# A one-core hybrid decoder layer: the last token block loaded and squared whole, the inverse roots' steps issued together, the parameter load on ScalarE's queue, and a new order of the projection jobs

## The chip, the cores and the metric

The kernel runs on one core of a Trainium2 chip. The metric is the device time of one execution in microseconds. The time of a kernel is the median of several runs; the kernel before took 1043.09 us (three runs, 1042.55 to 1043.57).

## The reference, cut to what matters

x has 512 tokens of 2048 features. One layer normalises x, projects it to 7824 columns, and feeds three token mixers; their gated outputs are joined, projected back, added to x and normalised again.

```python
h = _rmsnorm(x, norm_w[l])
p = h @ w_in[l]
y_a = _rwkv7_mix(...)   # 16 heads of 64: a chain over chunks of 64 tokens, then a norm over each head
y_b = _moba_mix(...)    # 4 heads of 128: causal softmax attention
y_c = _gla_mix(...)     # 4 heads: chunked linear attention with decay, then a norm over each head
mix = jnp.concatenate([y_a, y_b, y_c], axis=-1)
x = x + mix @ w_out[l]
return _rmsnorm(x, final_norm_w)
```

The first norm needs, for each token, the inverse root of the mean square of its 2048 features (`rstd`). The kernel projects the raw x (times the norm's weights) and multiplies each projected tile by `rstd` when it is taken out of PSUM.

## The kernel before, in words

**The stream.** TensorE runs one long stream of 128x128 by 128x512 products at float32 accuracy: weights and activations are each split into a high and a low part, and three products (high-high, high-low, low-high) replace one. 62 *jobs* of 128 output columns (`low` has 16) make the input projection: a job has 16 k-tiles, so 48 products. Then the output projection has four column blocks (`cb`) of 192 products. The first three jobs of `ORDER` run side by side, a quarter at a time, while x arrives.

**Banks.** Jobs take four PSUM banks (`gb`) in turn. So a job can begin only when the job four places before it in `ORDER` has been taken out of its bank (`evac`, line 378, a multiplication by `rstd` on VectorE). Each job is taken out by one particular step of the mixers (`wait_free`, line 1259, waits for it, and `force`, line 333, then runs mixer steps with no products between them).

**Side work.** The mixers are Python generators. `pump` (line 325) is called after every three products and lets each generator whose last step is thought to be finished issue its next step. What is "finished" comes from a clock of estimated costs (`Clock`, line 62), so the estimates and `ORDER` fix the program of every engine: the hardware then runs each engine's instructions in that order. Four other PSUM banks (`sbk`) serve the side work. The side work on TensorE that uses part of the array (64x64, 128x64, 32x32 operands, line 129) appears as short bursts in the stream; `bank` (line 351) may hold a step back for up to 4 us of the estimated clock to let it join a burst of its own form.

**The mixers' order.** RWKV runs four pairs of heads in turn (`rwkv(q)`, q = 0 to 3): preparation of `k` and `r` jobs, `a_stage`, `solve`, then `chain(q)` of eight chunks with three dependent bursts each, then `group_norm(q)`. `a_stage` of q waits for the end of `group_norm(q-1)` (flag `finish`), and that for the gate jobs `ga` of q-1. GLA (`gla(0)`, `gla(1)`) and then the attention heads (`moba(0)` to `moba(3)`) run one after the other in `others` (line 1044). `moba(h)` takes out `mq`, `mk` and `mv` of its head; `moba_gate(h)` (line 1037) takes out `mg` of head h only after head h-1 is done.

**The token norm.** `load` with kind "sq" (line 1123) loads a block of 128 tokens of x, untransposed; `square` (line 1151) squares it on ScalarE with a sum per token. Blocks 0 to 2 lie in one tile of 128x2048 each; block 3 lies in four tiles of 128x512 (`fb[0]` to `fb[3]`), has four loads and four squares, and its four sums go through `small`. `stats` (line 403) waits for the four squares, adds the four sums of block 3 (line 407), yields, then runs `rsqrt` (line 395: a scale and shift on VectorE, a power of -1/2 on GpSimd), transposes the result four times on TensorE (line 414) and copies it out to `rstd_b`. `rsqrt` serves the mixers' norms too; its GpSimd estimate is 0.1 us + 0.17 us per column.

**The start.** The parameters (line 1237) are the first load on the queue of the sync engine (SP), which issues almost all loads. The first activation on ScalarE needs them as a scale.

Of the kernel before, what the change touches and what calls it, by code (L numbers as in the profile page):

```python
# [12 lines left out]
AF = mybir.ActivationFunctionType  # L13
# [3 lines left out]
S, D = 512, 2048  # L17
# [5 lines left out]
NORM_EPS = 1e-6  # L23
# [13 lines left out]

ORDER = """wdad k0 k1 ga1 r0 ga0 r1 v0 gq0 low v1 gv0 gk0 k2 gg0 gv1 gg1 k3 r2 ga2 r3 gq1 v2 gk1 gg2 gv2 ga3 v3 gv3 gg3 k4 mq0 mk0 k5 r4 r5 ga4 v4 v5 mv0 mg0 k7 mq1 mk1 mg1 ga5 k6 mv1 r6 r7 mq2 ga6 mg2 v6 mk2 mv2 v7 mv3 mq3 mk3 ga7 mg3"""  # L40
FIRST = {"wdad": C_WD, "low": C_LOW, "k": C_K, "r": C_R, "v": C_V, "ga": C_GA, "gq": C_QC, "gk": C_KC, "gv": C_VC,
         "gg": C_GC, "mq": C_QB, "mk": C_KB, "mv": C_VB, "mg": C_GB}

# [1 line left out]
def first_column(job):  # L45
    kind = job.rstrip("01234567")
    return FIRST[kind] + 128 * int(job[len(kind):] or 0)


JOBS = [(n, first_column(n)) for n in ORDER.split()]  # L50

# [50 lines left out]
def tile_hybrid(ctx: ExitStack, tc: tile.TileContext, x, xT, wu, wlow, wout, par, cst, w2a2_d, aup_d, fw, out):  # L102
    nc = tc.nc
    ck = Clock()

    pool = ctx.enter_context(tc.tile_pool(name="main", bufs=1))
# [4 lines left out]
    def sb(name, shape, dt=F32, tag=None):  # L111
        t_ = pool.tile(list(shape), dt, name=name, tag=tag or name)
        return t_

    def numel(ap):
        n = 1
        for s in ap.shape[1:]:
            n *= s
        return n
# [15 lines left out]
    def tr(o, i):  # L135
        ck.pe(0.0925, "f")
        k = i.shape[0]
        nc.tensor.transpose(o, i, ident[:k, :k])  # L138

    def dcost(*aps):  # L140
        ps = any(a.space == bass.MemoryType.PSUM for a in aps if hasattr(a, "space"))
        return ((120 if ps else 60) + numel(aps[0])) / 960
# [14 lines left out]
    def ts(o, a, s1, s2, op0, op1=None):  # L157
        ck.add("dve", dcost(o, a) / 1.6)
        if op1 is None:
            nc.vector.tensor_scalar(o, a, s1, None, op0=op0)  # L160
        else:
            nc.vector.tensor_scalar(o, a, s1, s2, op0=op0, op1=op1)  # L162

    def vcopy(o, a):
        ck.add("dve", dcost(o, a) / 1.6)
        nc.vector.tensor_copy(o, a)  # L166

    def red(o, a, op=ALU.add):
        ck.add("dve", dcost(a, o))
        nc.vector.tensor_reduce(o, a, axis=AX.X, op=op)  # L170

    def act(o, a, f, bias=None, scale=None, accum=None, dep=0.0):
        t = TABLES.get(f)
        cost = 0.1 + numel(a) * 0.00084 + 0.1 * ((bias is not None) + (scale is not None))
        if t is not None and t != ck.table:
            ck.table = t
            cost += 1.3
        end = ck.add("act", cost, dep)
        kw = {}
        if bias is not None:  # L180
            kw["bias"] = bias
        if scale is not None:
            kw["scale"] = scale
        if accum is not None:
            kw["accum_out"] = accum
        nc.scalar.activation(o, a, f, **kw)  # L186
        return end
# [15 lines left out]
    params = sb("params", [128, NPAR])  # L203
# [40 lines left out]
    rst = gn[:, 1, 0:8]  # L244
# [23 lines left out]
    AWf = AW.rearrange("p a b c d -> p (a b c d)")  # L268
    BKtf = BKt.rearrange("p a b c -> p (a b c)")
    VSf, ARBf = (t.rearrange("p a b c d -> p (a b c d)") for t in (VS, ARB))  # L270
# [3 lines left out]
    squares = [0]  # L274
    fb = [sb(f"f{i}", [128, S]) for i in range(8)]

    xtok = [[(t, 0)] for t in (BKtf, VSf, ARBf)] + [[(fb[i], S * i) for i in range(4)]]
    fo = (fb[0], fb[2])
    att = sb("att", [128, 8, C])
    Sg = [sb(f"Sg{i}", [128, 128]) for i in range(2)]  # L280
    small = sb("small", [128, 48])

    gb = [psum.tile([128, 512], F32, name=f"gb{i}") for i in range(NGB)]
    sbk = [psum.tile([128, 512], F32, name=f"sb{i}") for i in range(8 - NGB)]
# [66 lines left out]
    def bank(n=1, tiling=None, patience=PATIENCE):  # L351

        if tiling is not None and ck.tiling != tiling:
            limit = ck.t["pe"] + patience
            yield lambda: ck.tiling == tiling or forcing[0] or ck.t["pe"] > limit
        if len(free_banks) < n:
            yield lambda: len(free_banks) >= n
        got = []
        for _ in range(n):
            b = min(free_banks, key=lambda b: bank_free[b])  # L360
            free_banks.remove(b)
            ck.cur.start = max(ck.cur.start, bank_free[b])
            got.append(b)
        if ck.cur.start + MARGIN > ck.t["pe"]:
            yield None
        return got[0] if n == 1 else got

    def release(i):
        bank_free[i] = ck.cur.ready
        free_banks.append(i)  # L370
# [24 lines left out]
    def rsqrt(v, r, scale, e):  # L395

        ts(v, v, scale, e, ALU.mult, ALU.add)
        n = numel(v)
        ck.add("pool", 0.1 + 0.17 * n)
        nc.gpsimd.tensor_tensor(r, v, mhalf[:, 0:n], op=ALU.pow)  # L400
        yield None

    def stats():
        yield lambda: squares[0] == 4
        ck.cur.start = max(ck.cur.start, ck.t["act"])
        yield None
        red(rst[:, 7:8], small[:, 0:4])
        yield None
        yield from rsqrt(rst[:, 4:8], rst[:, 0:4], 1.0 / D, NORM_EPS)
        ck.add("pool", 0.3)  # L410
        nc.gpsimd.tensor_copy(sel, consts[:, K_BD:K_BD + 130])
        b = yield from bank()
        for tb in range(4):
            tr(sbk[b][:, tb * 128:(tb + 1) * 128], rst[:, tb:tb + 1].to_broadcast([128, 128]))
        yield None
        vcopy(rstd_b, sbk[b])
        release(b)
        yield None
        flags["rstd"] = True
# [336 lines left out]
    def group_norm(q):  # L756
# [9 lines left out]
        red(gn[:, 1], ysq.rearrange("p (g n) -> p g n", n=C))  # L766
        yield None
        yield from rsqrt(gn[:, 1], gn[:, 2], 1.0 / C, GN_EPS)
        tt(y, y, gn[:, 2, :, None].to_broadcast([128, 16, C]), ALU.mult)
        yield None  # L770
# [77 lines left out]
    def gla(g):  # L848
# [105 lines left out]
        for i in range(2):  # L954
            act(fb[1], fo[i], AF.Square)
            yield None
            red(small[:, 8 + 4 * i:12 + 4 * i], t3(fb[1]))
        yield None
        yield from rsqrt(small[:, 8:16], small[:, 16:24], 1.0 / 128, NORM_EPS)
        for i in range(2):  # L960
            tt(t3(fo[i]), t3(fo[i]), small[:, 16 + 4 * i:20 + 4 * i, None].to_broadcast([128, 4, 128]), ALU.mult)
# [158 lines left out]
    def load(i):  # L1120
        kind, n = items[i]
        dep = 0.0
        if kind == "sq":

            rows = x[128 * n:128 * n + 128]
            for o, c in xtok[n]:
                nc.sync.dma_start(o, rows[:, c:c + numel(o)])
            ck.t["dma"] += 2.7
            load_end[i] = ck.t["dma"] + 2.0
            return  # L1130
        if kind == "x":
            o, src = xraw[n], xT[128 * n:128 * n + 128]
            ck.t["dma"] -= 0.07
        else:
            slot = slot_of[i]
            o = raws[slot % NRAW]
            if slot >= NRAW:
                dep = split_end[last_in_slot[slot - NRAW]]
            u = units[n]
            if u[0] == "in":  # L1140
                src = wu[tile_no[u[1]] * 4 + u[2]]
            elif u[0] == "low":
                o, src = o[:, 0:KT * 16], wlow
            else:
                k = K_ORDER[u[2]]
                src = wout[128 * k:128 * k + 128, 512 * u[1]:512 * u[1] + 512]
        nc.sync.dma_start(o, src)
        ck.t["dma"] = max(ck.t["dma"], dep) + 0.75
        load_end[i] = ck.t["dma"] + 2.0

    def square(tb, dep):

        for i, (o, _) in enumerate(xtok[tb]):
            act(o, o, AF.Square, accum=small[:, i:i + 1] if len(xtok[tb]) > 1 else rst[:, 4 + tb:5 + tb], dep=dep)
        squares[0] += 1

    mix_end, fetched, placed = {}, [0], [0]
# [76 lines left out]
        ck.t["pe"] = max(ck.t["pe"], split_end[item_of[u]] + 0.1)  # L1234


    nc.sync.dma_start(params, par)
    nc.gpsimd.memset(mhalf, -0.5)
    nc.scalar.activation(rst[:, 0:1], mhalf[:, 0:1], AF.Copy)
    nc.vector.memset(att, 0.0)  # L1240
# [7 lines left out]

    nc.gpsimd.memset(Pb[:, :, 0:1], 1.0)
    spawn("stats", stats())  # L1250
    spawn("start", start_track())
    nc.gpsimd.memset(Tt, 0.0)
# [10 lines left out]
    def job_bank(n):  # L1263
        nonlocal n_started
        if n not in in_bank:
            i = n_started % NGB
            n_started += 1
            old = bank_job[i]
            if old is not None:
                wait_free(old)  # L1270
            bank_job[i] = n
            in_bank[n] = gb[i]
            jobs[n].bank = gb[i]
        return in_bank[n]

    for u in range(n_in):
# [4 lines left out]
        kind, n, g = units[u]  # L1281
        o = job_bank(n)
# [165 lines left out]
```

## Time and profile before

| quantity | before |
|---|---|
| median of 3 runs | 1043.09 us |
| the profiled execution's own time | 1043.49 us |
| its span (first to last instruction) | 1041.8 us |
| mean granted TensorE clock | 0.998 |
| TensorE busy | 1025.5 us, 98% |
| VectorE busy | 656.9 us, 63% |
| ScalarE busy | 445.5 us, 43% |
| GpSimd busy | 49.7 us, 5% |

The span leaves out 1.69 us of the execution's own time. An engine's busy time is the time in which it had an instruction at work; matmul ends are modelled, so the distance from one start to the next is the safer measure of what a product costs.

### The profile page before, as it was taken

The numbers are of one execution on the slowest core, as the hardware profiler recorded it, in microseconds if no ns is written. First come the engines' busy times: TensorE is split into PE (matmuls) and PEld (weight loads), VectorE is DVE, ScalarE is ACT, GpSimd is POOL, SyncE is SP. The second block draws the span as 40 slices with busy tenths as digits, with TensorE's granted clock in tenths as the row PEclk, the third lists the DMA queues.
The fourth block names the chain that finished last, engine by engine and source line by source line (L and its number), as shares of the span: only waits on it lengthen the run. The fifth ranks groups of instructions, "written<-read, shape, count | busy, mean of one in ns | idle before, by whom it ended". The sixth has DMA issues, their size and how long they took to land.

```text
span 1041.8 us, 16696 instructions
## 1 busy us (share of the span) xinstructions
PE 1025.5 (98%) x6368; PEld 815.7 (78%) x6368; DVE 656.9 (63%) x1346; ACT 445.5 (43%) x790; POOL 49.7 (5%) x58
## 2 busy tenths in 40 slices
PE   7999999999999999999999999999999999999996
PEld 5788788777878877788888767888887788888885
DVE  5455689575777954765789565766975575424343
ACT  5665463352555334334544333454242274323323
POOL 0100000000200000020000001000000010202020
PEclk9999999999999999999999999999999999999999
DMA  9633233421433342233332322323341272443534
GB/s 329 213 97 92 63 109 94 108 61 46 136 102 92 91 117 62 61 102 117 91 92 87 105 69 81 112 79 105 94 110 52 63 282 87 136 141 93 168 115 162
DMA packets 80833, 115.02 MB, mean 110 GB/s; under 512 B 28257, under 2 KB 29473, under 8 KB 80241
## 3 DMA queue, kind: packets, MB, share of 16 engines
q1 hardware_dynamic: 80608, 112.90, 36.0%
q8 instruction: 50, 0.82, 0.3%
q0 software_dynamic: 144, 1.05, 0.3%
q14 instruction: 31, 0.25, 0.1%
HBM read 102.29 MB, written 11.63 MB: 109 GB/s over the span
## 4 chain that ended last, share of the span: by engine, by line
PE 94%; DMA 3%; ACT 1%; issue 1%; DVE 1%; POOL 0%; ACTq 0%; SPq 0%; POOLq 0%; DVEq 0%
PE gb L133 72%; PE sb L129 10%; PE sb L133 10%; PE sb L138 2%; DMA raw<-in_wu_dram 2%; DMA AW<-in_xT_dram 1%; ACT hi L186 0%; DVE lo L146 0%; ACT f L186 0%; DVE hlo L152 0%; ACT hhi L186 0%; POOL gn L400 0%; ACT ARB L186 0%; ACT pbuf L186 0%; DVE VS L146 0%
## 5 line engine op out<-in xcount | busy, mean ns | idle before, releaser
L133 PE MATMUL gb<-hhi,hi 128*128 128x512 f32 x976 | 399.0, 409 | 6.2 <-ACT hi L186 5.6
L133 PE MATMUL gb<-hhi,lo 128*128 128x512 f32 x976 | 382.8, 392 | 0.0
L133 PE MATMUL gb<-hlo,hi 128*128 128x512 f32 x976 | 382.2, 392 | 0.0
L186 ACT ACTIVATE hi<-raw 128x512 fp32r<-128x512 f32 x296 | 186.0, 630 | 391.1 <-PE gb L133 267.4
L146 DVE TENSOR_TENSOR lo<-raw,hi 128x512 fp32r<-128x512 f32 x296 | 208.3, 708 | 218.7 <-ACT hi L186 217.2
L133 PEld LDWEIGHTS gb<-hhi,hi 128*128 128x128 f32 x976 | 184.0, 189 | 50.5 <-ACT hi L186 5.6
L133 PEld LDWEIGHTS gb<-hhi,lo 128*128 128x128 f32 x976 | 183.9, 188 | 40.3 <-DVE lo L146 0.5
L133 PEld LDWEIGHTS gb<-hlo,hi 128*128 128x128 f32 x976 | 184.2, 189 | 34.2 <-DVE hlo L152 0.5
L146 DVE TENSOR_TENSOR scr<-scr 64x30 f32<-64x30 f32 (+14 forms) x240 | 77.4, 323 | 7.2
L133 PE MATMUL gb<-hi,hhi 128*128 128x512 f32 x128 | 50.3, 393 | 0.0
L133 PE MATMUL gb<-hi,hlo 128*128 128x512 f32 x128 | 49.9, 390 | 0.0
L133 PE MATMUL gb<-lo,hhi 128*128 128x512 f32 x128 | 49.8, 389 | 0.0
L186 ACT ACT_TABLE_LOAD x37 | 47.5, 1283 | 1.4 <-DVE f L882 0.7
L166 DVE COPY VS<-sb 64x128 f32<-64x128 f32 x64 | 18.5, 289 | 28.7 <-PE sb L129 27.6
L133 PE MATMUL sb<-hi,hhi 128*128 128x512 f32 x80 | 31.2, 389 | 0.0
L133 PE MATMUL sb<-lo,hhi 128*128 128x512 f32 x80 | 31.2, 389 | 0.0
L133 PE MATMUL sb<-hi,hlo 128*128 128x512 f32 x80 | 31.2, 389 | 0.0
L133 PE MATMUL sb<-late,hhi 128*128 128x512 f32 x96 | 30.2, 395 | 0.0
L186 ACT ACTIVATE f<-sb 64x256 f32<-64x256 f32 (+3 forms) x52 | 17.1, 362 | 29.3 <-PE sb L138 17.1
L400 POOL TENSOR_TENSOR gn<-gn,mhalf 128x16 f32<-128x16 f32 (+1 forms) x5 | 13.6, 2729 | 333.6 <-DVE gn L162 333.6
L186 ACT ACTIVATE Lt<-sb 64x256 f32<-64x256 f32 (+1 forms) x64 | 19.0, 323 | 24.0 <-PE sb L129 23.0
L133 PEld LDWEIGHTS gb<-hi,hlo 128*128 128x128 f32 x128 | 24.0, 188 | 5.0
(231 smaller groups left out, 1095.6 us busy)
## 6 DMA issues: line engine op xcount, KB each, us to landing
raw<-in_wu_dram SPq DMA_DIRECT2D x244, 256.0 KB
raw<-in_wout_dram SPq DMA_DIRECT2D x64, 256.0 KB
f<-in_x_dram SPq DMA_DIRECT2D x20, 256.0 KB
hlo<-mix SPq DMA_DIRECT2D x14, 256.0 KB
Ld<-Lt SPq DMA_DIRECT2D x4, 512.0 KB
mix<-f SPq DMA_DIRECT2D x7, 256.0 KB
mix<-ARB SPq DMA_DIRECT2D x7, 256.0 KB
AW<-in_xT_dram SPq DMA_DIRECT2D x6, 256.0 KB
```

Of the source, the lines that this page charges most:

```text
L129: nc.tensor.matmul(o, l, r, start=start, stop=stop, skip_group_check=skip)
L133: nc.tensor.matmul(o, l, r, start=start, stop=stop)
L138: nc.tensor.transpose(o, i, ident[:k, :k])
L146: nc.vector.tensor_tensor(o, a, b, op=op)
L166: nc.vector.tensor_copy(o, a)
L186: nc.scalar.activation(o, a, f, **kw)
L400: nc.gpsimd.tensor_tensor(r, v, mhalf[:, 0:n], op=ALU.pow)
```

## The change

x's fourth token block goes into one tile: the first 2048 columns of `AW`, which until then hold k-tiles 0 to 3 of the transposed x. It is loaded by one DMA and squared by one activation. The reduction of the four sums is gone with the yield after it, so the scale and shift follows at once; the sums and the roots swap places in `rst`. `rsqrt`'s GpSimd estimate rises by 0.5 us. The parameters are loaded from ScalarE's queue. `ORDER` is new: 62 jobs again, the first three are now `wdad k0 ga0` (before `wdad k0 k1`).

```diff
-ORDER = """wdad k0 k1 ga1 r0 ga0 r1 v0 gq0 low v1 gv0 gk0 k2 gg0 gv1 gg1 k3 r2 ga2 r3 gq1 v2 gk1 gg2 gv2 ga3 v3 gv3 gg3 k4 mq0 mk0 k5 r4 r5 ga4 v4 v5 mv0 mg0 k7 mq1 mk1 mg1 ga5 k6 mv1 r6 r7 mq2 ga6 mg2 v6 mk2 mv2 v7 mv3 mq3 mk3 ga7 mg3"""
+ORDER = """wdad k0 ga0 k1 r0 ga1 r1 v0 gq0 low v1 gv0 gk0 gg0 k2 gv1 k3 r2 gg1 ga2 gq1 v2 r3 gk1 ga3 gv2 v3 gg2 gv3 k5 k4 gg3 r4 mq0 r5 mg0 v4 ga4 mk0 v5 mv0 k7 mq1 k6 mg1 r6 r7 mv1 mk1 mg2 mq2 ga6 ga5 v6 v7 mk2 mv2 mq3 mv3 mk3 mg3 ga7"""
-    xtok = [[(t, 0)] for t in (BKtf, VSf, ARBf)] + [[(fb[i], S * i) for i in range(4)]]
+    xtok = [BKtf, VSf, ARBf, AWf[:, 0:D]]
-        ck.add("pool", 0.1 + 0.17 * n)
+        ck.add("pool", 0.6 + 0.17 * n)
-        red(rst[:, 7:8], small[:, 0:4])
-        yield None
-        yield from rsqrt(rst[:, 4:8], rst[:, 0:4], 1.0 / D, NORM_EPS)
+        yield from rsqrt(rst[:, 0:4], rst[:, 4:8], 1.0 / D, NORM_EPS)
-            tr(sbk[b][:, tb * 128:(tb + 1) * 128], rst[:, tb:tb + 1].to_broadcast([128, 128]))
+            tr(sbk[b][:, tb * 128:(tb + 1) * 128], rst[:, 4 + tb:5 + tb].to_broadcast([128, 128]))
-            for o, c in xtok[n]:
-                nc.sync.dma_start(o, rows[:, c:c + numel(o)])
+            nc.sync.dma_start(xtok[n], rows)
-        for i, (o, _) in enumerate(xtok[tb]):
-            act(o, o, AF.Square, accum=small[:, i:i + 1] if len(xtok[tb]) > 1 else rst[:, 4 + tb:5 + tb], dep=dep)
+        act(xtok[tb], xtok[tb], AF.Square, accum=rst[:, tb:tb + 1], dep=dep)
-    nc.sync.dma_start(params, par)
+    nc.scalar.dma_start(params, par)
```

## Rows read from the trace of the kernel before

**Rows 1.** The page's part 1: busy time, share of the span, instructions.

```profile
PE 1025.5 (98%) x6368; PEld 815.7 (78%) x6368; DVE 656.9 (63%) x1346; ACT 445.5 (43%) x790; POOL 49.7 (5%) x58
```

**Rows 2.** Table by stretches: length, then busy time of each engine, clock, DMA.

```profile
44.00:50.00 6.00, 4.77 (x24) 3.73 (x23) 2.02 (x6) 1.27 (x2) 2.39 (x5) 1.00 0.61 189
50.00:852.80 802.80, 802.59 (x5396) 633.93 (x5395) 556.61 (x1187) 348.73 (x620) 27.28 (x29) 1.00 0.33 94
```

**Rows 3.** Timeline of SP's queue at the start: start, length, instruction.

```profile
0.81 0.39 SPq L1237 DMA_DIRECT2D params<-in_par_dram  x1
1.26 0.42 SPq L1147 DMA_DIRECT2D AW<-in_xT_dram  x1
```

**Rows 4.** Timeline of ScalarE at the start; in brackets the idle time before and its releaser.

```profile
0.80 1.28 ACT L1239 ACT_TABLE_LOAD   x1 [0.80 <-PEq L1438]
...
4.27 0.72 ACT L186 ACTIVATE hhi<-AW,params 128x512 fp32r<-128x512 f32 x1 [1.98 <-DMA AW<-in_xT_dram]
```

**Rows 5.** Timeline of TensorE: the first product, and two at the early clock.

```profile
5.56 0.80 PE L133 MATMUL gb<-hhi,hi 128*128 128x512 f32 x1 [5.56 <-ACT hi L186]
...
12.20 0.63 PE L133 MATMUL gb<-hhi,hi 128*128 128x512 f32 x1
12.63 0.63 PE L133 MATMUL gb<-hlo,hi 128*128 128x512 f32 x1
```

**Rows 6.** Timeline of SP's queue: block 3's four loads.

```profile
21.87 3.84 SPq L1127 DMA_DIRECT2D f<-in_x_dram  x4
```

**Rows 7.** Timeline of ScalarE: the first of block 3's squares, and the next wait.

```profile
39.18 0.62 ACT L186 ACTIVATE f<-f 128x512 f32<-128x512 f32 x1
...
45.94 0.63 ACT L186 ACTIVATE hi<-raw 128x512 fp32r<-128x512 f32 x1 [2.50 <-DMA raw<-in_wu_dram]
```

**Rows 8.** Timeline of VectorE around the token norm.

```profile
44.10 0.15 DVE L170 TENSOR_REDUCE gn<-small 128x1 f32<-128x4 f32 x1
46.60 0.69 DVE L146 TENSOR_TENSOR lo<-raw,hi 128x512 fp32r<-128x512 f32 x1 [2.35 <-ACT hi L186]
47.22 0.16 DVE L162 TENSOR_SCALAR gn<-gn 128x4 f32<-128x4 f32 x1
```

**Rows 9.** Timeline of GpSimd and of TensorE: the power, and its transposes.

```profile
47.55 1.30 POOL L400 TENSOR_TENSOR gn<-gn,mhalf 128x4 f32<-128x4 f32 x1 [45.65 <-DVE gn L162]
...
48.91 0.65 PE L138 MATMUL sb<-consts,gn 128*128 128x128 f32 x4 [1.23 <-POOL gn L400]
```

**Rows 10.** Timeline of TensorE: a burst of 16 small products (GLA), one of 8 (RWKV).

```profile
182.37 0.68 PE L129 MATMUL sb<-f,f 64*64 64x64 f32 x16
182.98 0.50 PE L133 MATMUL gb<-hhi,hi 128*128 128x512 f32 x1
...
199.82 0.39 PE L133 MATMUL gb<-hhi,lo 128*128 128x512 f32 x1
200.14 0.45 PE L129 MATMUL sb<-VS,AW 64*64 64x64 f32 x8
200.52 0.50 PE L133 MATMUL gb<-hhi,hi 128*128 128x512 f32 x1
200.85 0.39 PE L133 MATMUL gb<-hlo,hi 128*128 128x512 f32 x1
```

**Rows 11.** The chain of waits: 192 products with nothing between them.

```profile
901.46 43.52 PE sb L133 x192
```

**Rows 12.** Timeline of VectorE: banks taken out, and the last steps of two heads.

```profile
668.48 0.68 DVE L146 TENSOR_TENSOR pbuf<-gb,rstd_b 128x512 f32<-128x512 f32 x1
...
716.94 0.68 DVE L146 TENSOR_TENSOR f<-f,f 128x512 f32<-128x512 f32 x1
...
721.11 0.67 DVE L146 TENSOR_TENSOR f<-gb,rstd_b 128x512 f32<-128x512 f32 x1
...
725.05 0.68 DVE L146 TENSOR_TENSOR f<-gb,rstd_b 128x512 f32<-128x512 f32 x1
...
831.92 0.69 DVE L146 TENSOR_TENSOR f<-gb,rstd_b 128x512 f32<-128x512 f32 x1
...
880.50 0.68 DVE L146 TENSOR_TENSOR f<-f,f 128x512 f32<-128x512 f32 x1
```

## The prediction, made before the changed kernel ran

> **What bounds the kernel now.** I read the page's busy times first: TensorE is at work for 1025.5 of 1041.8 us [rows 1], so only time that TensorE waits, or spends on something other than its products, can be won. Second, the table by stretches tells where it waits. From 50 to 852.8 us, the rest of the input projection with nearly all side work, it is idle for 802.80 - 802.59 = 0.21 us; from 44 to 50 us for 6.00 - 4.77 = 1.23 us [rows 2]. The other wait is the start: the first product begins at 5.56 us [rows 5]. Third, the timelines at these two places name the causes. At the start TensorE waits for ScalarE, which waits 1.98 us for the first tile of x [rows 4]; that load is second on SP's queue, behind the parameters [rows 3]. In the other place four transposes wait 1.23 us for GpSimd's power [rows 9]. Fourth, the timeline inside the stream shows what order can move: each burst of small products costs TensorE a fixed time beyond its products. It is worked out below.
>
> **Parameters on ScalarE's queue.** On SP the parameters' issue begins at 0.81 us, the first x tile's at 1.26 [rows 3]. Without it every load of the start is issued 1.26 - 0.81 = 0.45 us earlier, and the x tile that the first activation waits for lands 0.45 us earlier if it still takes as long. On ScalarE the issue now stands ahead of the table load (0.80 to 2.08). At SP's price of 0.39 us [rows 3] it ends some 0.4 us later, within the 1.98 us that ScalarE idles before 4.27, of which 1.5 are left after the earlier landing [rows 4]. If an issue on ScalarE cost over 1.5 us, the first activation would be late by the rest. I take -0.45. A first bound: in this stretch a product takes 12.63 - 12.20 = 0.43 us [rows 5], against 43.52 / 192 = 0.227 later [rows 11], TensorE's two clock levels, 1.2 and 2.4 GHz; the profile gives no granted clock of its own for those first microseconds. If the rise came no earlier than now, the 0.45 us won would hold 1.05 slow products, worth 1.05 x 0.227 = 0.24 us. So 0.24 to 0.45.
>
> The Trainium skill ("TensorE: Matmul & The Clock Gate", part 1, the clock gate) says that the window by which the clock is raised runs freely and does not restart with a kernel. By that rule the earlier start need not bring the rise forward, and the sum would have 0.24 in place of 0.45; no run here shows it yet.
>
> **Block 3 in one tile.** SP is freed of four issues, 3.84 us, for one [rows 6], and ScalarE of four squares of 0.62 us, each with its sum read out, for one longer square. I cost both at nothing. ScalarE's next wait after them is 2.50 us, for a weight load [rows 7], so a shorter square only lengthens it; and TensorE has no wait there but the one below. If that cover went, the price would be the difference of the squares, about half a microsecond. The new tile was read for the transposed x long before its load is issued (21.87 us), so the load takes on no new wait.
>
> **The inverse root's steps in a row.** Now the reduction runs on VectorE at 44.10 us, but the scale and shift only at 47.22: the yield let a split of weights in between, and that one waited 2.35 us for its load [rows 8]. GpSimd's power follows, 1.30 us, and the transposes start at 48.91 [rows 9]. In the new code the scale and shift stands where the reduction stood. With the same lag to GpSimd (47.55 - 47.22 = 0.33) the power ends near 44.10 + 0.33 + 1.30 = 45.7 us, before TensorE stopped in the old order (48.91 - 1.23 = 47.68). The higher estimate, 0.6 + 0.17 x 4 = 1.28 us against 0.78, now agrees with the 1.30 measured, and places the transposes 0.5 us later in TensorE's program. Both act against the wait. I take all of it: -1.23 us, bounds 0 and -1.23. Next late there is nothing: after 50 us TensorE waits 0.21 us in all [rows 2], so a microsecond won here stays won. In the mixers' norms the estimate only puts a step later, where TensorE waits for none of them; cost nothing.
>
> **The order.** The number of products is the same. What can change is the number of bursts, and banks that come free late. A burst of 16 lasts 182.98 - 182.37 = 0.61 us to the next big product, one of 8 lasts 200.52 - 200.14 = 0.38; so eight small products are worth 0.23 and 0.38 - 0.23 = 0.15 is fixed. The product before it takes 0.32 in place of 0.227, the one after 0.33 [rows 10, 11]. A burst costs 0.15 + 0.09 + 0.10 = 0.34 us beside its products. RWKV's chains make 4 x 8 x 3 = 96 dependent steps in either order, less the joint last ones; only GLA's bursts can join them or part from them. In the timeline I count seven that stand alone, the first at 182.37 [rows 10]. If all joined others: -2.4 us. If three more parted: +1.0. Nearer to now than to either end I take one burst fewer, -0.34: the second to fourth gate of GLA move by two or three places, its q, k and v jobs by at most one.
>
> **Sum.** -0.45 - 1.23 - 0.34 = -2.02 us: 1043.49 becomes 1041.47. The profiled execution lies 0.40 us above the median of the runs (1043.09), so against that median I expect 1041.1 us. That is 0.19% faster, almost at the 0.2% (2.1 us) that I take as the least a measurement of this kernel tells from no change.
>
> **Rival 1: a bank waits for a head.** In the new order `mk1` is job 49 (before 44) and `mg2` job 50 (before 53). `moba(1)` cannot finish without `mk1`, `mg2` is only taken out after `moba(1)`, and job 54 wants its bank. So a whole head must run inside the four jobs 50 to 53. In the old order the bank of job 49 was emptied at 668.48 and of job 53 at 725.05, four jobs in 56.57 us [rows 12]; four jobs alone are 43.52 us [rows 11]. The nearest head is the last, whose k, v and q were there together: from taking out `mk3` at 831.92 to its last product at 880.50 it took 48.58 us, and after head 1 the next bank was emptied 721.11 - 716.94 = 4.17 us after that product [rows 12]. 48.58 + 4.17 = 52.75 fits into 56.57, and is 9.2 us too long for the bare 43.52. For it: RWKV's last `a_stage` moves out of this stretch, since `ga5` goes from job 46 to 53, so the four jobs pass faster than 56.57. Against it: a head that is waited for runs without its patience of 4 us a step. I take no wait in the sum. From a wait of about 4.1 us on, the kernel is slower by over 0.2%; at 9.2 it takes 1041.1 + 9.2 = 1050.3, halfway (4.6) 1045.7.
>
> **Rival 2: the norm's wait stays.** The clock of estimates may again put a split that waits for its load ahead of the scale and shift, or the transposes too early. Then the change does not do there what it says, and the gain is -0.45 - 0.34: 1043.09 - 0.79 = 1042.3, no change. For it: the old code's clock already put a split with a late load in front [rows 8]. Against it: the reduction at 44.10 shows that VectorE's program had a free place before that split.
>
> **Rival 3: the order joins most lone bursts.** Then -0.45 - 1.23 - 2.4 = -4.1: 1039.0. For it: GLA's second gates come later and RWKV's jobs earlier, so that their bursts shift against each other. Against it: four of the seven lie before a chain can begin.
>
> **How the numbers follow.** The forecast has 0.60. Its own range is from -3 (two or three bursts joined) to -0.5 us, and a bit over half of it lies beyond -2.1: 0.33 faster, 0.27 no change. Rival 1 has 0.15, slower. Rival 2 has 0.13, no change. Rival 3 has 0.12, faster. Together faster 0.45, no change 0.40, slower 0.15. The range goes from rival 3 with a little more, 1038.3, through the forecast's 1040.1 to 1042.6, to a small bank wait, 1044.5; longer bank waits are left out.
>
> **What would show it.** Right: the first product near 5.1 us; VectorE's scale and shift near 44 us with no reduction before it; no idle time in front of the transposes; TensorE idle for well under a microsecond from 50 us to the output projection; about as many bursts as before. Wrong: a wait of TensorE near job 54, between 715 and 735 us, with VectorE's taking out of a bank as what ended it; an idle time before the transposes; or, with both gains there, a total that shows over three bursts more or fewer.

## The result: 0.5% slower, and the profile after

| quantity | before | after |
|---|---|---|
| median of 6 runs each, same chip | 1043.01 us (1042.46 to 1043.65) | 1048.55 us (1046.96 to 1050.27) |
| ratio after to before | | 1.0052, 95% interval 1.0042 to 1.0062 |
| the profiled execution's own time | 1043.49 us | 1049.31 us |
| its span | 1041.8 us | 1047.6 us |
| mean granted TensorE clock | 0.998 | 0.996 |

The kernel is 5.5 us slower where 2 us of gain were forecast; the time lies above the range.

First the two places where the gain was to come from. The timeline after, of ScalarE's first activation, of VectorE's first use of the parameters and of TensorE's first product (5.56 us in [rows 5]):

```profile
3.87 0.72 ACT L186 ACTIVATE hhi<-AW,params 128x512 fp32r<-128x512 f32 x1 [1.13 <-DMA params<-in_par_dram]
...
3.87 0.18 DVE L1239 TENSOR_SCALAR omu<-params 128x25 f32<-128x25 f32 x1 [2.40 <-DMA params<-in_par_dram]
...
5.16 0.80 PE L133 MATMUL gb<-hhi,hi 128*128 128x512 f32 x1 [5.16 <-ACT hi L186]
```

TensorE begins 0.40 us earlier. The same VectorE row of the kernel before, for the landing of the parameters:

```profile
2.65 0.18 DVE L1243 TENSOR_SCALAR omu<-params 128x25 f32<-128x25 f32 x1 [1.19 <-DMA params<-in_par_dram]
```

On ScalarE's queue the parameters are issued at 0.80 us and first used at 3.87; on SP they were issued at 0.81 [rows 3] and used at 2.65. They, no longer x's tile, now end the first activation's wait.

The table by stretches after (length, then busy time of each engine, clock, DMA share and GB/s), against [rows 2]:

```profile
44.00:50.00 6.00, 6.00 (x30) 4.92 (x29) 3.77 (x7) 3.69 (x6) 2.41 (x6) 1.00 0.68 207
50.00:850.00 800.00, 795.94 (x5359) 628.32 (x5358) 546.75 (x1170) 338.95 (x606) 26.24 (x26) 1.00 0.32 90
```

From 44 to 50 us TensorE is busy for all 6.00 us, so the norm's wait is gone. VectorE's scale and shift now comes 2.9 us earlier than in [rows 8], and the reduction before it is gone:

```profile
44.33 0.16 DVE L162 TENSOR_SCALAR gn<-gn 128x4 f32<-128x4 f32 x1
```

But from 50 to 850 us, where it was idle for 0.21 us, it is now idle for 800.00 - 795.94 = 4.06. TensorE's busy time hardly moves, from 1025.5 [rows 1] to 1026.7 on the page after:

```profile
PE 1026.7 (98%) x6368; PEld 815.4 (78%) x6368; DVE 656.0 (63%) x1345; ACT 443.4 (42%) x783; POOL 50.0 (5%) x58
```

The list of TensorE's waits after (what it waited for: us in all, times, longest) names two new ones, `xr` and `sgt`; the first row is the start (two rows are left out: 1.1 us for `hhi`, also at the start, and one of 0.2):

```profile
PE gb L133 <- ACT hi L186: 5.4, 2, 5.2
PE sb L133 <- DVE xr L146: 3.9, 1, 3.9
PE gb L133 <- DVE sgt L146: 1.7, 1, 1.7
```

**The first new wait, at 741 us.** The timeline of SP, of VectorE and of TensorE around it, engine by engine:

```profile
732.38 0.33 SPq L194 DMA_DIRECT2D Ld<-Lt  x1
735.02 1.92 SPq L194 DMA_DIRECT2D scr<-Ld  x4
...
734.94 0.68 DVE L146 TENSOR_TENSOR pbuf<-gb,rstd_b 128x512 f32<-128x512 f32 x1
740.31 1.22 DVE L146 TENSOR_TENSOR scr<-scr,n2l 64x1024 f32<-64x1024 f32 x1 [4.69 <-DMA scr<-Ld]
...
742.06 0.74 DVE L152 SCALAR_TENSOR_TENSOR vT<-pbuf,params,vT 128x512 f32<-128x512 f32 x1
742.72 2.02 DVE L146 TENSOR_TENSOR scr<-scr 64x30 f32<-64x30 f32 x8
744.67 0.68 DVE L146 TENSOR_TENSOR xr<-s,xr 128x512 fp32r<-128x512 f32 x1
...
741.13 0.39 PE L133 MATMUL sb<-xr,sel 128*128 128x512 f32 x1
745.40 0.79 PE L133 MATMUL sb<-xr,sel 128*128 128x512 f32 x1 [3.88 <-DVE xr L146]
745.99 0.63 PE L133 MATMUL gb<-hhi,hi 128*128 128x512 f32 x1
...
748.55 0.45 PE L133 MATMUL gb<-hhi,hi 128*128 128x512 f32 x1
```

Read it from SP down. `solve` of the last RWKV pairs stores `Lt` to `Ld` in HBM at 732.38 and gathers it back with four loads from 735.02 on. The product of the gathered tile with the norms (`scr<-scr,n2l`) is already next in VectorE's program behind the bank taken out at 734.94. It stands there idle for 4.69 us until the gather lands, and the steps of `pair_v`, which could have run before it (in `gather_late`, below, they do), stand behind it: `vT`, and `xr`, the low half of an operand. TensorE's second block-sum product needs that `xr` and starts 745.40 - 741.13 = 4.27 us after the first, where a product otherwise takes 0.227 [rows 11]: 4.04 us lost. Then the products follow at 0.43 us each. The table by stretches gives the granted clock of that piece:

```profile
745.40:748.50 3.10, 3.10 (x7) 2.47 (x8) 2.86 (x9) 0.63 (x1) 0.00 (x0) 0.50 0.29 87
```

0.50 is the lower level, 1.2 GHz. Seven products take 748.55 - 745.40 = 3.15 us instead of 7 x 0.227 = 1.59, so 1.56 us more. The wait costs 5.6 us in all.

In the kernel before the store was issued at 719.30 us and the same product stood at 728.23, 8.9 us later, behind splits of weights that TensorE needed sooner. It did not wait at all:

```profile
727.62 0.69 DVE L146 TENSOR_TENSOR lo<-raw,hi 128x512 fp32r<-128x512 f32 x1 [1.89 <-ACT hi L186]
728.23 1.21 DVE L146 TENSOR_TENSOR scr<-scr,n2l 64x1024 f32<-64x1024 f32 x1
```

**The second, at 861 us.** Timeline after, of GpSimd, ScalarE, VectorE and TensorE in turn:

```profile
850.60 0.76 POOL L1346 DMA_DIRECT2D AW<-in_fw_dram  x1
...
861.29 0.63 ACT L186 ACTIVATE hi<-raw 128x512 fp32r<-128x512 f32 x1 [4.93 <-DMA raw<-in_wout_dram]
...
861.95 0.69 DVE L146 TENSOR_TENSOR lo<-raw,hi 128x512 fp32r<-128x512 f32 x1 [3.37 <-ACT hi L186]
862.56 0.68 DVE L146 TENSOR_TENSOR sgt<-gb,rstd_b 128x512 f32<-128x512 f32 x1
...
861.24 0.39 PE L133 MATMUL gb<-hi,hlo 128*128 128x512 f32 x1
863.30 0.50 PE L133 MATMUL gb<-hi,hhi 128*128 128x512 f32 x1 [1.67 <-DVE sgt L146]
```

`ga7` is now the last job, and the output projection waits for its bank. It wants this bank last of the four, in its seventh group of three products, but that is only some 5 us after its first product at 856.02. VectorE takes it out (`sgt<-gb,rstd_b`) only behind a split of output weights whose load ScalarE awaited for 4.93 us. Meanwhile GpSimd's queue loads the final norm's weights, 1 MB, issued at 850.60. In the kernel before that issue came at 838.52, ahead of the loads of mixed outputs, which began at 841.41; now it falls among them. The stretch in question, in the table by stretches:

```profile
852.00:860.00 8.00, 8.00 (x39) 6.49 (x38) 6.54 (x13) 3.78 (x7) 0.00 (x0) 1.00 1.02 396
```

The DMA engines are full (share 1.02, 396 GB/s). TensorE's distance here is 863.30 - 861.24 = 2.06 us, 1.83 too long.

**Sum by the two traces.** Two waits, 5.6 + 1.83. The norm, -1.23. Two bursts of small products fewer (120 against 122, counted in the timelines), at the prediction's 0.34 each: -0.68. The 144th product, the last of the three side-by-side jobs, starts at 42.88 us against 42.53, so 0.35 later in spite of the early start. Together +5.9; the last product starts at 1038.60 us against 1032.72, also +5.9.

### The profile page after: what moved, and what is told of

Its sections match the earlier page's. It is cut to its first block, busy times and chain, and to the rows that moved or that the text cites. A ratio compares the mean times of both kernels' runs of the same rounds, so it can differ in the third digit from the quotient of the medians.

```text
span 1047.6 us, 16672 instructions
## 1 busy us (share of the span) xinstructions
PE 1026.7 (98%) x6368; PEld 815.4 (78%) x6368; DVE 656.0 (63%) x1345; ACT 443.4 (42%) x783; POOL 50.0 (5%) x58
## 4 chain that ended last, share of the span: by engine, by line
PE 92%; DMA 4%; DVE 1%; ACT 1%; issue 1%; SPq 0%; ACTq 0%; POOLq 0%; POOL 0%
PE gb L133 70%; PE sb L129 10%; PE sb L133 10%; PE sb L138 2%; DMA raw<-in_wu_dram 2%; DMA raw<-in_wout_dram 1%; DMA AW<-in_xT_dram 1%; ACT hi L186 0%; DVE lo L146 0%; SPq L1144 0%; ACT hhi L186 0%; DMA Ld<-Lt 0%; SPq L194 0%; ACT ARB L186 0%; DVE scr L146 0%
## 5 line engine op out<-in xcount | busy, mean ns | idle before, releaser
L133 PEld LDWEIGHTS gb<-hi,hhi 128*128 128x128 f32 x128 | 24.1, 188 | 7.0 <-DVE sgt L146 2.1
```

The lines of the kernel that those rows point to most:

```text
L133: nc.tensor.matmul(o, l, r, start=start, stop=stop)
```

## The experiments

The diffs are against the changed kernel unless said otherwise. A ratio is to the kernel before, timed beside it on the same chip.

### The edits without the order, and without the queue

`edits_only` is the changed kernel with the old `ORDER` line (the change's first diff line taken back); `edits_params_sp` also has the parameters back on SP:

```diff
-ORDER = """wdad k0 ga0 k1 r0 ga1
+ORDER = """wdad k0 k1 ga1 r0 ga0
...
-    nc.scalar.dma_start(params, par)
+    nc.sync.dma_start(params, par)
```

> The changed kernel with the old job order: block 3 in one tile, the inverse root's steps in a row, the parameters from ScalarE's queue. If the loss of 5.5 us comes from the order alone, these edits keep the early gain that the changed trace shows (the first burst of small products began at 120.01 us in place of 121.11), and the time is about 1041.9 us, 1.1 below the old kernel, with no wait of TensorE above 1 us after 14 us. If the edits themselves bring the late waits, for instance by the raised GpSimd estimate, the time is above 1043 us and a wait of several us stands between 700 and 870 us.

> The old order with all edits but one: the parameters go back to SP's queue. If ScalarE's queue gains time at the start, the first product begins 0.4 us later than with it (near 5.5 us in place of 5.14) and the time is about 0.4 us above that of the edits with the parameters on ScalarE, 1042.6 us; if the later landing of the parameters there (3.85 us in place of 2.65) eats the gain, the two times are the same. The norm's transposes wait for nothing in either case.

`edits_only` took 1042.18 us, ratio 0.9992 (0.9984 to 1.0001). `edits_params_sp` took 1042.68, ratio 1.0000 (0.9992 to 1.0009). All of TensorE's waits in `edits_only` but that for the start:

```profile
PE sb L129 <- DVE VS L166: 0.2, 1, 0.2
PE sb L133 <- DVE xr L146: 0.2, 1, 0.2
```

There is no late wait, and none for the norm in either run. So the loss belongs to the order, or to the order and the edits together. The shorter waits are in the traces. The runs show a gain of 0.8 us for `edits_only` (from 1.7 to -0.1 by its interval), where the prediction's two terms make 1.7, and none for `edits_params_sp`; the intervals of the two overlap, so they do not tell what the queue alone is worth. The section on the prediction says where a part of the gain goes.

### The order without the edits

`order_only` is the kernel before with the new `ORDER` line alone:

```diff
-ORDER = """wdad k0 k1 ga1 r0 ga0
+ORDER = """wdad k0 ga0 k1 r0 ga1
...
```

> The old kernel with the new job order and nothing else. If the order brings both late waits, TensorE stops again for about 4 us near 741 us behind VectorE's second part of xr and for 1 to 2 us near 861 us, the norm's wait of 1.2 us near 48 us stays, and the time is 1048.5 + 1.1 = about 1049.6 us. If the waits need the edits too, the time is near 1043 us.

It took 1055.59 us, ratio 1.0121 (1.0106 to 1.0137): slower than the changed kernel. TensorE's waits:

```profile
PE gb L133 <- DVE f L146: 4.6, 1, 4.6
PE sb L133 <- DVE xr L146: 3.7, 1, 3.7
PE gb L133 <- DVE sgt L146: 1.6, 1, 1.6
PE sb L138 <- POOL gn L400: 1.1, 1, 1.1
```

Both new waits are there without the edits, and the norm's wait of the old code too. And a third appears, 4.6 us at 185 us: TensorE stands before `gv1` until VectorE has taken `gv0` out of its bank, in a pair of steps from 188.00 on, and then runs seven products at 0.43 us. Ahead of that pair VectorE works on steps of a `solve`; the product with `sq` among them starts at 184.59, in the changed kernel at 179.49. The excess over the changed kernel is 0.0121 - 0.0052 = 0.0069 of 1043, 7.2 us. Its parts are 1.1 (the norm), 4.6, and 7 x 0.2 = 1.4 for the slow products: 7.1, and from the 144th product to the last the trace of `order_only` takes 1002.82 us against 995.71, 7.1 more. Three more bursts (123 against 120) ought to add 1.0 and do not show; the parts are an account, not a proof. The wait for `gv0` was not foreseen: about 1049.6 us was expected. The same order thus gives another program with the old code, since the edits also shift the clock of estimates (the GpSimd estimate, the yield); which of them keeps the wait away was not tried alone.

### The gather: too early in VectorE's program, or too slow?

The theory: `solve` issues its product too early. `dma` (line 189) prices a transfer from the end of the generator's own last step, but `solve` reads tiles that other generators (`a_stage`) have just written, so the price starts from an old time. `gather_late` lets it start from ScalarE's estimated time, for the last solve alone. The rival: the gather is slow because SP's queue or its transfers hold it; `gather_pool` issues store and gather from GpSimd's queue.

```diff
     def solve():
+        if ck.cur.name == "rwkv3":
+            ck.cur.start = max(ck.cur.start, ck.t["act"])
         dma(Ld, Lt)
```

```diff
-        dma(Ld, Lt)
+        eng = nc.gpsimd if ck.cur.name == "rwkv3" else None
+        dma(Ld, Lt, eng=eng)
...
-                    lands=6.0)
+                    lands=6.0, eng=eng)
```

> The changed kernel; only the estimated clock of the last solve is set right: its store of Lt starts no earlier than ScalarE's estimate, so its product with the norms is issued later on VectorE and other steps stand ahead of it. Theory 1 (VectorE stands in line behind a product whose gather has not landed): the wait of 3.9 us near 741 us goes, with the slow products behind it, about 5.6 us, and the time is about 1043 us. Theory 2 (the weight load stands behind the gathers on SP's queue): TensorE still waits about 2 us there, since VectorE's split of these weights could not begin before 741.4 us; about 1045.5 us. The wait near 861 us stays under both, unless the shift of some 5 us moves it.

> The changed kernel with the last solve's store of Lt and its four gathers issued from GpSimd's queue in place of SP's, so that no weight load stands behind them; VectorE's order around them is kept. Theory 1: VectorE still waits for the gather, 4.7 us or more, and TensorE about 4 us or more near 741 us: 1048.5 us or above. Theory 2: the weight load lands some 3 us earlier and the wait near 741 us shrinks below 1 us: about 1043 us.

`gather_late` took 1042.37 us, ratio 0.9994 (0.9984 to 1.0003). Of the late waits only `sgt` is left, 1.5 us. Its timeline, SP and then VectorE:

```profile
731.16 0.33 SPq L194 DMA_DIRECT2D Ld<-Lt  x1
...
734.03 1.92 SPq L194 DMA_DIRECT2D scr<-Ld  x4
...
733.72 0.69 DVE L146 TENSOR_TENSOR pbuf<-gb,rstd_b 128x512 f32<-128x512 f32 x1
735.83 0.69 DVE L146 TENSOR_TENSOR lo<-raw,hi 128x512 fp32r<-128x512 f32 x1 [1.43 <-ACT hi L186]
736.44 0.75 DVE L152 SCALAR_TENSOR_TENSOR vT<-pbuf,params,vT 128x512 f32<-128x512 f32 x1
737.10 0.68 DVE L146 TENSOR_TENSOR xr<-s,xr 128x512 fp32r<-128x512 f32 x1
...
742.35 1.21 DVE L146 TENSOR_TENSOR scr<-scr,n2l 64x1024 f32<-64x1024 f32 x1
```

The gathers follow the store by 2.87 us (2.64 in the changed kernel), but behind `pbuf` VectorE now goes on with splits, `vT` and `xr`, and the product comes at 742.35, with no wait. Two lines of bookkeeping, which change no instruction, only their places, win 0.0058, 6.0 us.

`gather_pool` took 1048.22 us, ratio 1.0052 (1.0039 to 1.0066). Timeline of GpSimd and VectorE:

```profile
731.27 0.76 POOL L194 DMA_DIRECT2D Ld<-Lt  x1 [61.40 <-ACT Lt L186]
734.66 2.55 POOL L194 DMA_DIRECT2D scr<-Ld  x4 [2.64 <-DMA Ld<-Lt]
...
740.02 1.22 DVE L146 TENSOR_TENSOR scr<-scr,n2l 64x1024 f32<-64x1024 f32 x1 [5.79 <-DMA scr<-Ld]
```

From store to product it is 740.02 - 731.27 = 8.75 us, against 740.31 - 732.38 = 7.93 on SP, and the wait for `xr` is 5.0 us long (that for `sgt` 0.7, in place of 1.7). The rival falls: here the round trip through HBM takes some 8 us from either queue, and what removes the wait is a place behind other work.

### The weights of the final norm

`fw_sp` loads them from SP's queue; `both` is `gather_late` with that edit.

```diff
-                    nc.gpsimd.dma_start(fwt, fw.rearrange("(o d) -> o d", o=1).to_broadcast([128, D]))
+                    nc.sync.dma_start(fwt, fw.rearrange("(o d) -> o d", o=1).to_broadcast([128, D]))
```

> The changed kernel with the final norm's weights loaded from SP's queue and nothing else; the instructions of the four other engines stand as in the changed kernel. If that load is the cause of the second wait, TensorE's 1.7 us near 861 us go and the 3.9 us near 741 us stay: 1048.5 - 1.8 = about 1046.7 us. If not, 1048.5 us.

> The changed kernel with two repairs: the last solve's product placed late on VectorE, as in the run before, and the final norm's weights (1 MB) loaded from SP's queue, where their place in the program comes after the mixes' loads, in place of GpSimd's queue, where they start as soon as the last chain has read AW. If the second wait (1.5 us near 856 us, VectorE taking out the last gate job behind a split whose weights land late) comes from this load in the middle of the mixes, it goes, and the time is 1042.4 - 1.7 = about 1040.7 us. If the mixes' own 14 loads fill the DMA engines anyway, the wait stays and the time is 1042.4 us.

`fw_sp` took 1046.28 us, ratio 1.0035 (1.0023 to 1.0047); the `sgt` wait is gone and `xr` is the one wait of TensorE over 0.2 us behind the first three jobs:

```profile
PE sb L133 <- DVE xr L146: 3.5, 1, 3.5
```

In the changed kernel, then, the second wait goes when that load is moved. `both` took 1042.23 us, ratio 0.9993 (0.9984 to 1.0002), no better than `gather_late`: the `sgt` wait is still 1.5 us long. Its timeline of VectorE shows another cause:

```profile
852.74 2.50 DVE L146 TENSOR_TENSOR hlo<-hlo,hhi 128x512 fp32r<-128x512 f32 x4
...
855.76 0.68 DVE L146 TENSOR_TENSOR sgt<-gb,rstd_b 128x512 f32<-128x512 f32 x1
```

Here no load is late. Four subtractions of mixed outputs (2.50 us) and a split stand ahead of `ga7`'s bank. So a wait at this place has two possible causes, and what they share is that the last job's bank is wanted back some 5 us after that job's products end, while VectorE prepares the output projection's operands.

### The place of ga5: rival 1 by itself

`ga5_early` puts `ga5` back to job 46 in the new order.

```diff
...
-mg1 r6 r7 mv1 mk1 mg2 mq2 ga6 ga5 v6 v7
+mg1 ga5 r6 r7 mv1 mk1 mg2 mq2 ga6 v6 v7
...
```

> The changed kernel with the gate job ga5 moved from place 53 to place 46, where the old order had it, and the rest of the new order kept. If the loss comes from the last a_stage and the v6 steps starting together behind ga5, the wait of VectorE for the gather goes and with it TensorE's 3.9 us near 741 us; the four jobs in which head 1 must finish are then three, and TensorE may wait 1 to 3 us for the bank of mg2 near 742 us. 1042 to 1046 us. If the loss comes from elsewhere in the new order, the wait stays and the time is 1048 us or above.

It took 1049.95 us, ratio 1.0069 (1.0055 to 1.0083). The gather's wait is gone; TensorE and VectorE at another place:

```profile
737.64 1.71 PE L133 MATMUL sb<-xr,sel 128*128 128x512 f32 x2 [4.31 <-ACT xr L186]
740.73 0.79 PE L133 MATMUL gb<-hhi,hi 128*128 128x512 f32 x1 [1.38 <-DVE f L146]
...
739.99 1.28 DVE L146 TENSOR_TENSOR f<-gb,rstd_b 128x512 f32<-128x512 f32 x2
```

VectorE takes `mg2`'s bank out at 739.99, after the last steps of head 1. TensorE has nothing but side steps from `v6`'s last product (732.04) to `v7`'s first (740.73), waits 4.31 + 1.38 us among them, and runs at 0.43 us per product until 746.1. By its bank and its place this is rival 1. It is not head 1 alone that fills it: the 4.31 us are ended by ScalarE's `xr` of `v6`, whose own bank VectorE took out only at 735.64, behind steps of `solve`. Against `gather_late` the run costs 0.0069 + 0.0006 = 0.0075, 7.8 us, and it lies above the 1042 to 1046 us expected. So `ga5` at job 53 avoids one wait and makes the other.

### The last two jobs, and the two repairs together

`late_tail` is `gather_late` with `ga7 mg3` as the last two jobs, as before the change. `both_tail` is `both` with that edit. `order_late` is `order_only` with `gather_late`'s edit.

```diff
...
-mv3 mk3 mg3 ga7"""
+mv3 mk3 ga7 mg3"""
```

> The changed kernel with the last solve's gather priced by ScalarE's estimated clock (as in gather_late) and the last two jobs in the old order, ga7 mg3. Theory 'the last job's bank': the wait of 1.5 us near 855 us stands because ga7 is the last job, and its bank is taken out by the RWKV norm while VectorE splits the output projection's weights; with mg3 last again, the wait shrinks below 0.5 us (the kernel before had none there) and the time is 1042.4 - 1.3 = about 1041.1, ratio 0.9985. Rival theory 'the weights of the final norm': the wait is set by the late 1 MB load on GpSimd's queue; then it stays near 1.5 us in front of whichever block uses that bank, and the time stays at 1042.4. Third possibility: mg3's bank itself comes late by the 0.9 us that the planner's estimate has there (857.35 to 858.21); then about 1041.8.

> The same as late_tail, with the final norm's weights loaded from SP's queue as well. If the last job's bank alone makes the wait near 855 us, this gives what late_tail gives, about 1041.1. If the 1 MB load alone makes it, late_tail stays at 1042.4 and this stays at 1042.2, since the load moved alone did not end the wait. If both are needed, only this run falls to about 1041.

> The kernel before with the new order alone (order_only, 1055.6) and the gather priced late. If the wait at 747 us in order_only has the same cause as in the changed kernel, it goes, and with it 3.7 us of waiting and 1.5 us of low clock: 1055.6 - 5.5 = about 1050. The wait of 4.6 us at 185 us for the bank of gv0 stays, since the planner forces it. If the two have different causes, the xr wait stays and the time stays near 1055.

`late_tail` took 1040.65 us, ratio 0.9982 (0.9973 to 0.9991), below both kernels. `both_tail` took 1041.03, ratio 0.9985 (0.9976 to 0.9994): the queue of the 1 MB load makes no difference once the last bank is right. All of TensorE's waits in `late_tail`:

```profile
PE gb L133 <- ACT hi L186: 5.8, 2, 5.2
PE sb L129 <- DVE VS L166: 0.2, 1, 0.2
PE gb L133 <- DVE f L146: 0.2, 1, 0.2
```

Behind the first three jobs nothing over 0.2 us is left. `order_late` took 1050.08 us, ratio 1.0072 (1.0057 to 1.0087), 0.0049 or 5.1 us below `order_only`, and only the gather's wait is missing from its list (but for the start):

```profile
PE gb L133 <- DVE f L146: 4.6, 1, 4.6
PE gb L133 <- DVE sgt L146: 1.5, 1, 1.5
PE sb L138 <- POOL gn L400: 1.0, 1, 1.0
```

So the gather's wait has the same cause, with or without the edits.

## Why the prediction was wrong, point by point

- **What bounds the kernel** was read rightly: TensorE's idle time and its bursts. The page cannot show, though, how near to late a step without a wait already stands.
- **Parameters on ScalarE's queue, -0.45 (0.24 to 0.45).** The step was right at the first product: 5.13 to 5.35 us in the nine executions with ScalarE's queue, 5.52 to 5.82 in the four with SP's. Its reason was not: the parameters now land later and take x's place as what the activation waits for. How much of it lasts is not shown. The 144th product starts at 41.23 to 42.88 us with ScalarE's queue and 41.65 to 42.53 with SP's; the means, 41.9 and 42.1, are 0.2 us apart in a spread of 1.6. That lies nearer to the lower bound of 0.24, but so few traces tell it neither from 0 nor from 0.45.
- **The clock at the start.** The last product at the slow spacing starts at 13.1 us before and 11.1 after, and anywhere from 8.6 to 13.1 in all thirteen traces, 3.4 to 7.5 us behind the first product: the rise does not follow the first product at a fixed distance. The Trainium skill ("TensorE: Matmul & The Clock Gate", part 1, the clock gate) says that the window runs freely and does not restart with a kernel; these traces fit that, without singling it out, since TensorE's early waits differ between them too. In the mean the last slow product starts at 10.1 us with ScalarE's queue and 11.7 with SP's, so whether the earlier start brings the rise forward is open. An early rise can be given back in part: in `ga5_early` it came at 8.7 us, and then TensorE stood before a weight's split for 1.46 us, until 30.51.
- **Block 3 in one tile, nothing.** Nothing shows against it: TensorE waits for its load or its square in no run.
- **The inverse root's steps in a row, -1.23.** Right, in size and place; rival 2 did not happen. From the 144th product to the 193rd the ten kernels with the new code take 11.57 to 11.67 us, the one before 13.03, so 1.4 less. In `order_only` and `order_late`, with the old code, the wait is still 1.1 and 1.0 us. But "a microsecond won here stays won" was too strong: `edits_params_sp` has this gain and is at 1.0000 (0.9992 to 1.0009). From the 193rd main product to the last one the kernel before takes 1032.72 - 55.56 = 977.16 us, `edits_only` 1030.89 - 53.06 = 977.83. The new program of the old order costs 0.67 us more on the way (`edits_params_sp`, with 977.81, 0.65), though it has one burst fewer.
- **The order, -0.34.** Here it failed. The burst count was nearly right (two fewer, not one). The failing sentence is "What can change is the number of bursts, and banks that come free late". A third thing changes: behind which transfer another step stands on its engine. Moving `ga5` seven places moves `finish(2)`, and with it `a_stage(3)` and `solve` to the moment at which `pair_v` of `v6` runs (with `ga5` back at its place this wait is gone); `solve`'s store and gathers were never counted. The term that was put at nothing cost 5.6 us there and 1.83 at the last job's bank. The kernel before had the distance on show: 8.9 us from store to product, with no wait because other splits filled them. The same goes for the last job's bank and the 1 MB load that starts when the side work ends.
- **Rival 1** named nearly the right stretch (715 to 735 us, job 54; the wait stands at 741, in job 55) and the wrong mechanism. In the changed kernel `mg2`'s bank is not waited for. What was written in the rival's favour, that `a_stage` leaves the stretch, is what saved that bank; it arrived at the next place instead. With `ga5` at its old place rival 1's bank wait happens, at 7.8 us beside the 9.2 worked out; the nearness is in part luck, since steps of `solve` and `pair_v` stand in that wait too.
- **The sum.** Without the two new waits the total holds: `late_tail` has the edits, the two bursts fewer and no late wait, and its ratio is 0.0018 of 1042.7, 1.9 us (0.9 to 2.8) below the kernel before; -2.02 was forecast. That it comes so near is in part luck. From the 193rd main product to the last `late_tail` takes 976.87 us, 0.96 less than `edits_only` with the old order, where one burst fewer (120 against 121) makes 0.34; that makes up for the 0.67 which the edits lose there. What was wrong is "I take no wait in the sum", and the 0.15 for all ways of being slower.

What stays open: why the old code with the new order waits for `gv0` was not traced to one edit, nor what the edits lose 0.67 us to with the old order.

## What to carry to other kernels

In a program whose order is fixed ahead, ask of every reordered step what stands behind it on its engine and which transfer it waits for; a long round trip that shows no wait today is hidden by the order, not free. When a planner fixes the order, look at where its estimate of a transfer begins: a start taken from a step's own last action misses what other steps wrote. Swap in a new order one moved job at a time, since two late steps can take turns at being hidden.

## What was not expected of the hardware

- The same small parameter load is first used 1.84 us after its issue from SP's queue and 3.07 us after it from ScalarE's, where x's first tile is issued 0.01 us later on SP. Whether the queue or the company makes the difference was not tried.
- A wait of 3.9 us in the middle of a full stream costs more than itself: the granted clock is 0.50 behind it for 3.1 us, 1.56 us more. In `order_only`, behind 4.6 us, it is seven products at 0.43 us; in `order_late`, behind a wait of the same 4.6 us at the same place, twelve; in `ga5_early`, behind two waits, twelve. So the price of one wait is not fixed.
- Kernels with the same program up to 600 us differ in when TensorE's clock rises (8.7 us in `gather_pool`, 11.8 in `gather_late`) and by up to 1.65 us in when the 144th product starts (41.23 in `both_tail`, 42.88 in the changed kernel). Here a gain of some tenths at the start can be judged only over many runs.
